# A fused layer's last down-projection as seven block products instead of eight, with its operands' sums made during the up-projections

## The chip, the core and the metric

The kernel runs on one core of a Trainium2 chip. Its engines run side by side: TensorE (PE, with PEld for its weight loads), VectorE (DVE), ScalarE (ACT), GpSimd (POOL) and SyncE (SP), which here issues every DMA between DRAM and the on-chip memory (SBUF). PE writes its results into PSUM banks of 128x512 fp32. The metric is the device time of one execution in microseconds (us), a median of several.

## The reference

One layer: a SwiGLU feed-forward block, two attentions with a merge, and a second SwiGLU block, for 1024 latent tokens of width 1024 (and 256 context tokens ahead of the second block). What the change touches is the second block, with 2816 inner columns:

```python
def _swiglu(h, w1, w3, w2):
    return (jax.nn.silu(h @ w1) * (h @ w3)) @ w2
...
x = _residual(x, _swiglu(_modnorm(x, g[4], m[6], m[7]), ffn2_w1[l], ffn2_w3[l], ffn2_w2[l]),
              g[5], m[8], HALF_STEP)
```

`_residual` normalises each token's row, multiplies by a gate row and adds `x`. All is fp32. To keep fp32's precision in PE's faster format (`fp32r`), each operand is split into a high part (an ACT cast) and the rest (a DVE subtraction), and each product is three matmuls: high by high, high by low, low by high (`mm3`, line 158).

## The kernel before

The **order** comes from a `Plan` (line 163): a list of main steps that hold the matmuls of a stage, and side steps that `spread` lays evenly behind a range of main steps. All engines take their instructions in the order in which this plan writes them. A `store` made in a main step is put on SP's queue two steps later (`waiting`, `flush`); a load goes on at once, and whatever stands in SP's queue is issued in order.

The **up-projections** of the second block (`up_units`, `Unit`, `plan_rest`) work on pairs of inner tiles of 128. For each pair there are two units, one for w1 and one for w3; 11 pairs make 22 units. Each unit multiplies a 2 x 2 block matrix of weights by one of tokens (h's halves) in seven products instead of eight, with sums of the weight blocks made by DVE (`sum`), splits of these by ACT and DVE, and results combined from PSUM banks by DVE. One product is one main step of 12 matmuls (4 inner steps of 3). The first 14 units are led: their products `first` and `second` are done earlier, and five products, p6, p5, p7, p3, p4, are left to them; the last 8 units have all seven. `plan_rest` thus has 14 x 5 + 8 x 7 = 126 main steps. The w1 unit's results go through a Silu on ACT (`emit1`), the w3 unit's are multiplied with them by DVE (`emit3`) and stored, by halves of 512 tokens, to the DRAM buffer `gd2` (one 128x1024 tile for each of the 22 inner tiles).

The **pools** concerned: `T2()` gives tiles of 128x512 from the pool `half`, which has 20; in the rows below they are named `t`. `xu` are tiles of the pool `units` (24), `xv` of the pool `wide` (16), `d` are DRAM buffers. The PSUM banks are `bs` (3), `bm` (3) and `bv` (2). A tile is given out again once its last reader is done, a DMA too.

The **down-projection** (`Down`, `groups`) works on groups of inner tiles, nine of two and one of four. For each tile it loads 512 KB of w2 and 512 KB of `gd2` and splits both. A main step `tile(t)` takes one token tile of 128 (8 of them) and both output halves `e`; for each it runs 3 matmuls per inner tile of the group into a bank:

```python
for x, f in enumerate(fs):
    mm3(pd, [y[:, c] for y in g[f]], self.w[f][e], x == 0, x == len(fs) - 1)
if fs[0] == 0:
    act.copy(ys[t][:, o], pd)
else:
    vec.tensor_tensor(ys[t][:, o], ys[t][:, o], pd, op=ALU.add)
```

So each of 10 groups ends with 16 evictions of 128x512: for the first group a copy by ACT, for the others an addition to `ys[t]` by DVE. Beside it run the steps of the last modulation column (`ada_steps((8,))`, 16 loads `in_wada` and 16 small matmuls), its gate rows (`last_gates`), and in the last group the residual of each token tile in two halves (`done2`: statistics, gate, the addition of `x2s`, the store of the output).

Of the kernel before, what the change touches and what calls it, by code (L numbers as in the profile page):

```python
# [43 lines left out]
def hybrid_block(ctx: ExitStack, tc: tile.TileContext, a: dict, out: bass.AP):  # L44
# [25 lines left out]
    def V(dt=F32):  # L70
        return U(dt, "v")
# [4 lines left out]
    def T2(dt=F32, n=512):  # L76
        return pools["t"].tile([P, n], dt, tag="t", name=nm("t"))
# [4 lines left out]
    def DR(shape):  # L82
        n = nm("d")
        return dp.tile(shape, F32, tag=n, name=n)
# [3 lines left out]
    def PB(tag):  # L88
        return ps.tile([P, 512], F32, tag=tag, name=nm("b" + tag), bufs=PBUFS[tag])
# [22 lines left out]
    class Engine:  # L112


        def __init__(self, e):
            self.e = e
# [93 lines left out]
    def load(src, n=1024, key="u"):  # L210
        r = U(key=key)[:, :n]
        ld(r, src)
        return r
# [133 lines left out]
    def gate_rows(col, key="u"):  # L347
        row = U(key=key)
        for h in range(2):
            pb = PB("s")  # L350
# [239 lines left out]
    def plan_rest(plan, units):  # L590

        for i, u in enumerate(units):
            o = len(plan.main)
            e = plan.step(*u.rest())
            at = lambda n: o + u.names.index(n)
            for n, f in (u.within() if i else []) + (units[i + 1].before() if i + 1 < len(units) else []):
                plan.spread([f], at(n), at(n) + 1)
            if i + 2 < len(units):
                plan.spread([lambda v=units[i + 2], x=x: v.load(x) for x in (2, 0, 1)], e - 3, e)
# [54 lines left out]
                plan.spread([f], at[t] + x, at[t] + x + 1)  # L654


    def up_units(h, w1, w3, gd):

        units = []

        def pair_(p):
            s = {}

            def emit1(i, ci, x, bank):
                s[i, ci] = T2() if bank else x
                act.activation(s[i, ci], x, AF.Silu)

            def emit3(i, ci, x, bank):
                y = s.pop((i, ci))
                vec.tensor_tensor(y, x, y, op=ALU.mult)  # L670
                store(gd[2 * p + i, :, ci * 512:(ci + 1) * 512], y)
# [1243 lines left out]
    def last_col():  # L1915
        cols["g8"] = gate_col(8, 5, 0, 0.5)

    def last_gates():
        cols["g8"] = gate_rows(cols["g8"], "v")
# [109 lines left out]
```

## Time and profile before

| | us |
|---|---|
| median of 3 runs | 2691.38 |
| lowest and highest run | 2686.49, 2692.72 |
| the profiled execution, span on the core | 2689.4 |
| rest of the second block's up-projections | about 2096 to 2439 |
| its down-projection, first to last matmul | 2438.94 to 2681.0 |

The page puts the profiled execution in 40 equal slices, each digit the busy share in tenths:

```profile
PE   7999999999999999999999999999999999999998
DVE  4777875586866676665457988885535777565876
PEclk9999999999999999999999999999999999999999
GB/s 289 153 170 136 149 107 118 145 168 108 159 116 97 224 209 155 154 268 216 232 295 258 258 99 75 75 17 198 71 110 184 137 130 114 71 94 195 118 94 125
```

A slice is 67 us; the second block's part discussed here is the last nine slices. PEclk is the clock that TensorE was granted, and GB/s what all DMA engines moved. In the groups of instructions that come later, a row gives line, engine, operation, output and inputs, shapes and count, then busy time and mean duration in ns, then the idle time of the engine just ahead of them with the engine that ended it. In a timeline a row starts with the start and the duration.

### The profile page before, as it was taken

What the parts mean: (1) busy time and instruction counts of PE and PEld (TensorE: products, weight loads), DVE (VectorE), ACT (ScalarE), POOL (GpSimd) and SP (SyncE); (2) the same over time, 40 slices, a digit from 0 to 9 for tenths busy, and PEclk for the clock granted to TensorE, in tenths of its full rate; (3) what the DMA queues carried; (4) which work ended last, traced back from release to release, by engine and by line L of the source; (5) the groups of instructions that cost most, each with busy time, mean ns of one, the idle gap of its engine ahead of it and who ended that gap; (6) DMA issues with size and microseconds to landing.
All of it is one profiled execution on the core that took longest, in us unless ns stands there. A gap on an engine that the chain in (4) does not pass through costs nothing.

```text
span 2689.4 us, 37823 instructions
## 1 busy us (share of the span) xinstructions
PE 2638.9 (98%) x13822; PEld 2259.5 (84%) x13822; DVE 1838.0 (68%) x3443; ACT 1136.2 (42%) x2168; POOL 230.8 (9%) x380
## 2 busy tenths in 40 slices
PE   7999999999999999999999999999999999999998
PEld 5888888888898788799888999997788888888887
DVE  4777875586866676665457988885535777565876
ACT  5522233522223753331447987773256322324111
POOL 0000000000000400000103532221020000000001
PEclk9999999999999999999999999999999999999999
DMA  7454433453432654476889942205235433225323
GB/s 289 153 170 136 149 107 118 145 168 108 159 116 97 224 209 155 154 268 216 232 295 258 258 99 75 75 17 198 71 110 184 137 130 114 71 94 195 118 94 125
DMA packets 186154, 409.69 MB, mean 152 GB/s; under 512 B 21680, under 2 KB 60784, under 8 KB 185968
## 3 DMA queue, kind: packets, MB, share of 16 engines
q1 hardware_dynamic: 185968, 407.27, 46.8%
q8 instruction: 109, 1.79, 0.3%
q14 instruction: 77, 0.63, 0.1%
HBM read 308.04 MB, written 99.16 MB: 151 GB/s over the span
## 4 chain that ended last, share of the span: by engine, by line
PE 52%; issue 33%; ACT 6%; DVE 6%; DMA 2%; POOL 1%; SPq 0%; DVEq 0%; POOLq 0%; ACTq 0%
PE bs L153 23%; PE bm L153 15%; PE bv L153 11%; PE bm L156 2%; ACT xu L1648 1%; DVE t L120 1%; DVE xu L1515 1%; DVE xu L120 1%; ACT xu L1549 1%; POOL st L120 1%; DVE xv L120 1%; ACT t L120 1%; ACT t L1674 1%; DVE t L1675 1%; ACT xu L120 1%
## 5 line engine op out<-in xcount | busy, mean ns | idle before, releaser
L153 PE MATMUL bm<-xu,xu 128*128 128x512 f32 (+2 forms) x2304 | 551.4, 388 | 1.4 <-DVE xu L120 1.1
L153 PEld LDWEIGHTS bm<-xu,xu 128*128 128x128 f32 x2304 | 426.0, 189 | 84.8 <-DVE xu L120 1.9
L153 PE MATMUL bs<-xu,xu 128*128 128x512 f32 (+1 forms) x1908 | 459.5, 386 | 0.6 <-DVE xu L120 0.4
L153 PEld LDWEIGHTS bs<-xu,xu 128*128 128x128 f32 x1908 | 354.6, 189 | 69.7 <-DVE xu L120 0.9
L153 PE MATMUL bs<-xv,xu 128*128 128x512 f32 (+1 forms) x1488 | 355.7, 389 | 4.7 <-DVE t L120 4.6
L153 PEld LDWEIGHTS bs<-xv,xu 128*128 128x128 f32 x1488 | 279.6, 189 | 62.2 <-issue 6.3
L153 PE MATMUL bv<-xv,xu 128*128 128x512 f32 x1276 | 318.5, 389 | 0.0
L120 ACT CAST xu<-t 128x512 fp32r<-128x512 f32 x248 | 150.8, 616 | 335.6 <-DVE t L120 332.9
L153 PEld LDWEIGHTS bv<-xv,xu 128*128 128x128 f32 x1276 | 239.6, 188 | 49.8
L120 DVE TENSOR_TENSOR xu<-t,xu 128x512 fp32r<-128x512 f32 x248 | 170.5, 689 | 136.3 <-ACT xu L120 136.3
L120 DVE TENSOR_TENSOR xu<-xv,xu 128x512 fp32r<-128x512 f32 (+2 forms) x244 | 182.8, 770 | 63.3 <-ACT xu L120 60.1
L120 POOL TENSOR_SCALAR st<-st 128x1 f32<-128x1 f32 x72 | 41.6, 577 | 2104.4 <-ACT t L120 2038.7
L153 PE MATMUL bs<-w,w 96*128 96x512 f32 (+3 forms) x832 | 206.1, 366 | 7.7 <-DVE st L1540 7.1
L120 DVE TENSOR_TENSOR xu<-xu,xu 128x512 fp32r<-128x512 f32 (+2 forms) x225 | 154.4, 692 | 76.8 <-ACT xu L120 74.7
L120 ACT CAST xu<-xv 128x512 fp32r<-128x512 f32 (+2 forms) x216 | 137.2, 694 | 125.4 <-DVE xv L120 108.6
L153 PE MATMUL bm<-t,xu 128*128 128x256 f32 (+1 forms) x1272 | 167.3, 289 | 0.6 <-ACT t L120 0.4
L153 PEld LDWEIGHTS bm<-t,xu 128*128 128x128 f32 x1272 | 162.3, 193 | 5.7 <-ACT t L120 0.8
L153 PE MATMUL bv<-xu,xu 128*128 128x512 f32 x596 | 160.4, 391 | 0.0
L153 PE MATMUL bv<-t,w 128*128 128x256 f32 x896 | 151.2, 288 | 5.0 <-ACT t L1674 1.7
L153 PEld LDWEIGHTS bv<-t,w 128*128 128x128 f32 x896 | 132.6, 189 | 20.6 <-DVE t L1675 5.0
L120 ACT CAST xu<-xu 128x512 fp32r<-128x512 f32 (+2 forms) x217 | 131.9, 621 | 29.2 <-DMA xu<-in_wc 18.1
L153 PEld LDWEIGHTS bs<-w,w 96*128 96x128 f32 (+1 forms) x832 | 123.2, 190 | 17.1 <-DVE st L1540 10.1
(187 smaller groups left out, 3674.8 us busy)
## 6 DMA issues: line engine op xcount, KB each, us to landing
d<-t SPq DMA_DIRECT2D x244, 256.0 KB, 2.4
xu<-in_f1w SPq DMA_DIRECT2D x64, 512.0 KB, 4.1
xv<-in_f1w SPq DMA_DIRECT2D x64, 512.0 KB, 3.7
xv<-d SPq DMA_DIRECT2D x62, 512.0 KB, 4.2
xu<-in_f2w SPq DMA_DIRECT2D x60, 512.0 KB, 3.9
t<-in_wada SPq DMA_DIRECT2D x112, 256.0 KB, 3.9
w<-d SPq DMA_DIRECT2D x112, 256.0 KB, 6.5
t<-d SPq DMA_DIRECT2D x76, 256.0 KB, 4.1
```

The source lines that it names most:

```text
L120: return lambda *x, **y: pin(f(*x, **y))
L153: return pin(nc.tensor.matmul(o, s, m, start=start, stop=stop, skip_group_check=open_group[0]))
L156: return pin(nc.tensor.transpose(o, x, i))
L1515: nc.vector.tensor_scalar(dst, src, 1.0, FMIN, op0=ALU.mult, op1=ALU.max, accum_out=m)
L1549: soft.append(lambda s=s: nc.scalar.activation(pr[s][:, :640], pr[s][:, :640], AF.Exp, bias=n_[:, s:s + 1], accum_out=l[:, s:s + 1]))
L1648: nc.scalar.activation(x, x, AF.Exp, bias=n_[:, s:s + 1], accum_out=l[:, i:i + 1])
L1674: nc.scalar.copy(t[0], pb)
L1675: nc.vector.tensor_tensor(t[1], pb, f32(t[0]), op=ALU.subtract)
```

## The change

The down-projection is written as the product of a 2 x 2 block matrix A (rows: token halves of 512; columns: even and odd inner tile of each pair) and a 2 x 2 block matrix W (rows: even and odd inner tile; columns: output halves of 512). It needs seven products of blocks: with s1 = a21 + a22, s2 = s1 - a11, s3 = a11 - a21, s4 = a12 - s2 and t1 = w12 - w11, t2 = w22 - t1, t3 = w22 - w12, t4 = w21 - t2, these are a11 w11, a12 w21, s2 t2, s1 t1, s4 w22, s3 t3 and a22 t4.

- `Quarters` holds the token blocks: where a w3 unit's result was stored to `gd2`, a11, a12 and a22 are now stored each to a buffer of its own, and a21 is kept. The four sums of a pair (one DVE operation and one store each) stand behind the steps p5, p7, p3, p4 of the next pair's w1 unit if that is led, else behind its second to fifth step. For the 7 led pairs a11 is loaded again (`back`) ahead of that. The last pair's sums stand in the down-projection's first steps.
- `WeightQuarters` loads for each pair the four blocks of w2 (256 KB each), makes t1 to t4 with four DVE subtractions and stores them: six side steps for each of 11 pairs, laid evenly over the 126 main steps but four.
- `Down7` has 77 steps (7 products by 11 inner steps), each with 4 token tiles of 3 matmuls, into four banks; operands are loaded six steps ahead (two pieces of 256 KB) and split three steps ahead. Products that are added to one another stay in their banks, so a bank is read after each product only: 28 evictions. The last 5 inner steps of the last product are done token tile by token tile (`tail`, 15 matmuls each), as before the last group.
- The modulation's steps, its gate rows and `done2` are placed anew; the gate rows use the banks `bv` instead of `bs`.

```diff
+    def plan_quarters(plan, quarters, p, o):
...
+        def run(x):
+            if not made:
+                made.extend(quarters.steps(p))
+            made[x]()
+        for x in range(4):
+            plan.spread([lambda x=x: run(x)], o + x + 1, o + x + 2)
...
+            if quarters:
+                if i % 2 and u.led:
+                    plan.spread([lambda p=i // 2: quarters.back(p)], o, o + 1)
+                elif i % 2 == 0 and i:
+                    plan_quarters(plan, quarters, i // 2 - 1, o)
...
+    class Quarters:
...
+        def take(self, p, i, ci, y):
+            n = "a" + "12"[ci] + "12"[i]
+            self.y[p][n] = y
+            if n != "a21":
+                store(self.d[n][p], y)
...
+        def back(self, p):
+            t = self.y[p]["a11"] = T2()
+            ld(t, self.d["a11"][p])
...
+            def s1():
+                y["s1"] = T2()
+                vec.tensor_tensor(y["s1"], y["a21"], y["a22"], op=ALU.add)
+                store(self.d["s1"][p], y["s1"])
+            def s3():
+                vec.tensor_tensor(y["a21"], y["a11"], y["a21"], op=ALU.subtract)
+                store(self.d["s3"][p], y["a21"])
+            def s2():
+                vec.tensor_tensor(y["a11"], y["s1"], y["a11"], op=ALU.subtract)
+                store(self.d["s2"][p], y["a11"])
+            def s4():
+                vec.tensor_tensor(y["a12"], y["a12"], y["a11"], op=ALU.subtract)
+                store(self.d["s4"][p], y["a12"])
+                self.y[p] = None
+            return [s1, s3, s2, s4]
...
+    class WeightQuarters:
...
+        def load(self, p):
+            for n in ("w11", "w12", "w22", "w21"):
+                t = self.r[p, n] = T2()
+                ld(t, self.src(n, p))
...
+        def sums(self, p):
+            w = {n: self.r.pop((p, n)) for n in ("w11", "w12", "w22", "w21")}
+            def one(n, x, y, out):
+                vec.tensor_tensor(w[out], w[x], w[y], op=ALU.subtract)
+                store(self.d[n][p], w[out])
+            return [lambda a=a: one(*a) for a in (("t1", "w12", "w11", "w11"), ("t3", "w22", "w12", "w12"),
+                                                  ("t2", "w22", "w11", "w22"), ("t4", "w21", "w22", "w21"))]
...
+                s += [lambda p=p: self.load(p), lambda: None] + [lambda x=x, run=run: run(x) for x in range(4)]
...
+    class Down7:
...
+        ORDER = (("a11", "w11"), ("a12", "w21"), ("s2", "t2"), ("s1", "t1"), ("s4", "w22"), ("s3", "t3"), ("a22", "t4"))
+        TAIL = 5
...
+        def load(self, i):
+            (a, w), k = self.ORDER[i // NP], i % NP
+            self.r[i] = T2(), T2()
+            ld(self.r[i][0], self.q.d[a][k])
+            ld(self.r[i][1], self.wq.src(w, k))
+        def split(self, i, x):
+            self.w.setdefault(i, []).append(split(self.r[i][x]))
+            if x:
+                self.r.pop(i)
...
+        def product(self, i, t):
+            open_group[0] = True
+            o, k = i // NP, i % NP
+            a, w = self.w[i]
+            mm3(self.banks[t], [x[:, t * P:(t + 1) * P] for x in a], w, k == 0 and o in (0, 2, 3), k == NP - 1)
...
+        def step(self, i):
+            o, k = i // NP, i % NP
+            if k == 0:
+                if o == 0:
+                    self.xb = self.banks = [PB(x) for x in "smsm"]
+                if o == 2:
+                    self.yb = self.banks = [PB(x) for x in "smvv"]
+                if o == 3:
+                    self.xb = self.banks = [PB(x) for x in "smsm"]
+                if o == 4:
+                    self.banks = self.xb
+                if o == 5:
+                    self.banks = self.yb
+            for t in range(4):
+                self.product(i, t)
+            self.w.pop(i)
+            if k == NP - 1:
+                for t in range(4):
+                    self.out(o, t)
+        def out(self, o, t):
+            b, lo, hi = self.banks[t], slice(0, 512), slice(512, 1024)
+            ys = self.ys
+            if o == 0:
+                ys[t + 4] = V()
+                act.copy(ys[t + 4][:, lo], b)
+            elif o == 1:
+                ys[t] = V()
+                act.copy(ys[t][:, lo], b)
+            elif o == 2:
+                vec.tensor_tensor(ys[t][:, hi], b, ys[t + 4][:, lo], op=ALU.add)
+            elif o == 3:
+                vec.tensor_tensor(ys[t + 4][:, hi], b, ys[t + 4][:, lo], op=ALU.add)
+            else:
+                y = (ys[t][:, hi], ys[t + 4][:, hi], ys[t + 4][:, lo])[o - 4]
+                vec.tensor_tensor(y, y, b, op=ALU.add)
+        def tail(self, t):
+            for i in range(self.n - self.TAIL, self.n):
+                self.product(i, t)
+            self.out(6, t)
+        def plan(self, plan, ahead=6, led=3):
+            o = len(plan.main)
+            plan.step(*[lambda i=i: self.step(i) for i in range(self.n - self.TAIL)])
+            e = len(plan.main)
+            plan.step(*[lambda t=t: self.tail(t) for t in range(4)])
+            for i in range(self.n):
+                at = o + i - led
+                if i >= self.n - self.TAIL:
+                    at = e - 2 * (self.n - i)
+                plan.spread([lambda i=i: self.load(i)], at - ahead + led, at - ahead + led + 1)
+                plan.spread([lambda i=i, x=x: self.split(i, x) for x in range(2)], at, at + 1)
...
+                if quarters:
+                    quarters.take(p, i, ci, y)
+                else:
+                    store(gd[2 * p + i, :, ci * 512:(ci + 1) * 512], y)
...
-    gd2 = DR([NF, P, NLAT])
-    units2 = up_units(h3, a["f2w1"], a["f2w3"], gd2)
+    quarters2, wq2 = Quarters(), WeightQuarters(a["f2w2"])
+    units2 = up_units(h3, a["f2w1"], a["f2w3"], None, quarters2)
...
-    plan_rest(plan, units2)
-    gs = groups((2,) * 9 + (4,))
+    rest2 = len(plan.main)
+    plan_rest(plan, units2, quarters2)
+    plan.spread(wq2.steps(), rest2, len(plan.main) - 4)
     ys2 = {}
-    downs2 = [Down(a["f2w2"], gd2, ys2, fs) for fs in gs]
-    o = len(plan.main)
-    plan.spread([lambda: downs2[0].loads(0, "u")], o - 9, o - 8)
-    plan.spread(downs2[0].steps(key="u"), o - 7, o)
+    down2 = Down7(quarters2, wq2, ys2, None)
+    o, tail = down2.plan(plan)
+    plan_quarters(plan, quarters2, NP - 1, o)
...
-    d2_at = len(plan.main)
-    for i, d in enumerate(downs2):
-        o = len(plan.main)
-        plan.step(*[lambda d=d, t=t: d.tile(t) for t in range(8)])
-        if i + 1 < len(downs2):
-            n = downs2[i + 1]
-            plan.spread([lambda n=n: n.loads(n.fs[0])], o - 1, o)
-            plan.spread(n.steps(), o + 1, o + 8)
-        else:
-            plan.spread([last_col], o - 3, o - 2)
-            plan.spread([last_gates], o - 1, o)
-            for t in range(8):
-                plan.spread([lambda t=t: done2(t, 0)], o + t, o + t + 1)
-                plan.spread([lambda t=t: done2(t, 1)], min(o + t + 1, o + 7), o + 8)
-    plan.spread(ada_steps((8,)), d2_at + 8, len(plan.main) - 20)
+    plan.spread(ada_steps((8,)), o + 1, o + 2 * NP - 3)
+    plan.spread([last_col], o + 2 * NP - 3, o + 2 * NP - 2)
+    plan.spread([last_gates], o + 2 * NP - 2, o + 2 * NP - 1)
+    for t in range(4):
+        plan.spread([lambda t=t, x=x: done2(t, x) for x in range(2)], o + 5 * NP + 2 * t, o + 5 * NP + 2 * t + 2)
+        plan.spread([lambda t=t: done2(t + 4, 0)], tail + t, tail + t + 1)
+        plan.spread([lambda t=t: done2(t + 4, 1)], min(tail + t + 1, tail + 3), tail + 4)
```

Three places show how instructions move. First DVE, in the rest of a led w1 unit, from a sum for p7's bank on. Names: `t` are half tiles, `bs` and `bv` banks, `xu` the split weights. Before:

```order
L120 TENSOR_TENSOR t_21539<-t_21539,bs_21505 128x512
L120 TENSOR_TENSOR t_21561<-xu_21502,t_21544 128x512
L120 TENSOR_TENSOR xu_21563<-t_21561,xu_21563 128x512
L120 TENSOR_TENSOR t_21518<-t_21518,bv_21526 128x512
L120 TENSOR_TENSOR xu_21582<-t_21544,xu_21582 128x512
L120 TENSOR_TENSOR t_21585<-xu_21502 128x512
L120 TENSOR_TENSOR t_21361<-t_21361,bs_21505 128x512
L120 TENSOR_TENSOR xu_21603<-t_21585,xu_21603 128x512
L120 TENSOR_TENSOR t_21621<-bs_21608,t_21462 128x512
```

After, at the same products of a led w1 unit one pair earlier:

```order
L120 TENSOR_TENSOR t_21361<-t_21361,bs_21327 128x512
L120 TENSOR_TENSOR t_21084<-t_21232,t_21084 128x512
L120 TENSOR_TENSOR t_21394<-xu_21322,t_21368 128x512
L120 TENSOR_TENSOR xu_21396<-t_21394,xu_21396 128x512
L120 TENSOR_TENSOR t_21340<-t_21340,bv_21348 128x512
L120 TENSOR_TENSOR t_21232<-t_21363,t_21232 128x512
L120 TENSOR_TENSOR xu_21416<-t_21368,xu_21416 128x512
L120 TENSOR_TENSOR t_21419<-xu_21322 128x512
L120 TENSOR_TENSOR t_21174<-t_21174,bs_21327 128x512
L120 TENSOR_TENSOR t_21127<-t_21127,t_21232 128x512
L120 TENSOR_TENSOR xu_21439<-t_21419,xu_21439 128x512
L120 TENSOR_TENSOR t_21370<-t_21372,t_21370 128x512
L120 TENSOR_TENSOR t_21459<-bs_21446,t_21280 128x512
```

Four rows are new. The three token sums s3, s2 and s4 (`t_21084`, `t_21232`, `t_21127`) stand between the products' bank reads (rows with `bs` or `bv`) and the splits (rows with `xu`) as listed; s1 is `t_21363`, four rows ahead of these. `t_21370<-t_21372,t_21370` is a weight difference.

Second PE, where the down-projection starts. Rows with x2 and x3 are as many matmuls of one form. Before, a bank gets two inner tiles (6 matmuls) and PE goes on to the other output half, with two token halves of a split weight:

```order
L153 MATMUL bm_23622<-xu_23496,xu_23539 128x512 x2
L153 MATMUL bm_23622<-xu_23496,xu_23540 128x512
L153 MATMUL bm_23622<-xu_23561,xu_23596 128x512 x2
L153 MATMUL bm_23622<-xu_23561,xu_23597 128x512
L153 MATMUL bv_23630<-xu_23519,xu_23539 128x512 x2
L153 MATMUL bv_23630<-xu_23519,xu_23540 128x512
L153 MATMUL bv_23630<-xu_23578,xu_23596 128x512 x2
L153 MATMUL bv_23630<-xu_23578,xu_23597 128x512
```

After, each inner step gives 3 matmuls to each of four banks, and comes back to the first:

```order
L153 MATMUL bs_23909<-xu_23853,xu_23850 128x512 x3
L153 MATMUL bm_23910<-xu_23853,xu_23850 128x512 x3
L153 MATMUL bs_23911<-xu_23853,xu_23850 128x512 x3
L153 MATMUL bm_23912<-xu_23853,xu_23850 128x512 x3
L153 MATMUL bs_23909<-xu_23877,xu_23874 128x512 x3
L153 MATMUL bm_23910<-xu_23877,xu_23874 128x512 x3
L153 MATMUL bs_23911<-xu_23877,xu_23874 128x512 x3
L153 MATMUL bm_23912<-xu_23877,xu_23874 128x512 x3
```

A bank that was closed after 6 matmuls now stays open for 11 or 22 inner steps. Over the whole program PE's rows go from 10885 to 10489, DVE's from 3114 to 3166, ACT's from 1902 to 1982 and SP's from 1207 to 1445.

Third SP's queue early in the down-projection, where `in_f2w` is w2, `d` a DRAM buffer (`d_19714` is `gd2`, `d_19715` holds a11) and `in_wada` the modulation's weights. Before:

```order
L132 DMA xv_23680<-d_19714 128x1024
L132 DMA xv_23781<-in_f2w 128x1024
L132 DMA xv_23783<-d_19714 128x1024
L132 DMA t_23803<-in_wada 128x512
L132 DMA xv_23843<-in_f2w 128x1024
L132 DMA xv_23845<-d_19714 128x1024
L132 DMA t_23847<-in_wada 128x512
L132 DMA t_23889<-in_wada 128x512
L132 DMA xv_23946<-in_f2w 128x1024
```

After:

```order
L132 DMA t_24091<-in_f2w 128x512
L132 DMA t_24095<-in_wada 128x512
L132 DMA d_19720<-t_23638 128x512
L132 DMA t_24116<-d_19715 128x512
L132 DMA t_24117<-in_f2w 128x512
L132 DMA t_24121<-in_wada 128x512
L132 DMA t_24124<-in_wada 128x512
L132 DMA t_24144<-d_19715 128x512
L132 DMA t_24145<-in_f2w 128x512
L132 DMA t_24149<-in_wada 128x512
```

Transfers of 128x1024 have become twice as many of 128x512, and the stores of the last sums stand among them.

More of the change, by code (lines that the diff above doesn't have):

```diff
@@ L588, in plan_leads, with plan_rest @@
         plan.step(*lead_main(units[:n]))
-    def plan_rest(plan, units):
+    def plan_quarters(plan, quarters, p, o):
+        made = []
+        def run(x):
[4 more added lines that the diff above has]
+            plan.spread([lambda x=x: run(x)], o + x + 1, o + x + 2)
+    def plan_rest(plan, units, quarters=None):
         for i, u in enumerate(units):
@@ L654, in plan_chains, with __init__, steps @@
                 plan.spread([f], at[t] + x, at[t] + x + 1)
-    def up_units(h, w1, w3, gd):
+    class Quarters:
+        def __init__(self):
+            self.d = {n: DR([NP, P, 512]) for n in ("a11", "a12", "a22", "s1", "s2", "s3", "s4")}
+            self.y = [{} for _ in range(NP)]
+        def take(self, p, i, ci, y):
[6 more added lines that the diff above has]
+            ld(t, self.d["a11"][p])
+        def steps(self, p):
+            y = self.y[p]
+            def s1():
[13 more added lines that the diff above has]
+            return [s1, s3, s2, s4]
@@ new lines, in hybrid_block, with __init__, src, steps @@
+    class WeightQuarters:
+        def __init__(self, w2):
+            self.w2 = w2
+            self.d = {n: DR([NP, P, 512]) for n in ("t1", "t2", "t3", "t4")}
+            self.r = {}
+        def src(self, n, p):
+            if n[0] == "t":
+                return self.d[n][p]
+            o = 512 * (int(n[2]) - 1)
+            return self.w2[2 * p + int(n[1]) - 1][:, o:o + 512]
+        def load(self, p):
[9 more added lines that the diff above has]
+                                                  ("t2", "w22", "w11", "w22"), ("t4", "w21", "w22", "w21"))]
+        def steps(self):
+            s = []
+            for p in range(NP):
+                made = []
+                def run(x, p=p, made=made):
+                    if not made:
+                        made.extend(self.sums(p))
+                    made[x]()
+                s += [lambda p=p: self.load(p), lambda: None] + [lambda x=x, run=run: run(x) for x in range(4)]
+            return s
@@ new lines, in hybrid_block, with __init__ @@
+    class Down7:
+        ORDER = (("a11", "w11"), ("a12", "w21"), ("s2", "t2"), ("s1", "t1"), ("s4", "w22"), ("s3", "t3"), ("a22", "t4"))
+        TAIL = 5
+        def __init__(self, q, wq, ys, done):
+            self.q, self.wq, self.ys, self.done = q, wq, ys, done
+            self.r, self.w = {}, {}
+            self.n = NP * len(self.ORDER)
+        def load(self, i):
[12 more added lines that the diff above has]
+            mm3(self.banks[t], [x[:, t * P:(t + 1) * P] for x in a], w, k == 0 and o in (0, 2, 3), k == NP - 1)
+            open_group[0] = False
+        def step(self, i):
[48 more added lines that the diff above has]
+                plan.spread([lambda i=i, x=x: self.split(i, x) for x in range(2)], at, at + 1)
+            return o, e
@@ L659, in up_units @@
+    def up_units(h, w1, w3, gd, quarters=None):
         units = []
```

7 lines of the change are left out of this document (3 added, 4 removed).

## The prediction

> **What bounds the kernel now.** First the page's top: the busy shares over the whole span.
>
> ```profile
> span 2689.4 us, 37823 instructions
> PE 2638.9 (98%) x13822; PEld 2259.5 (84%) x13822; DVE 1838.0 (68%) x3443; ACT 1136.2 (42%) x2168; POOL 230.8 (9%) x380
> ```
>
> The tensor engine (PE) is busy for 98%, but that is a mean over stages with different limits, so I read the windows of the stages that the change touches. The columns are: the window, its length, then busy time and count of PE, PEld, DVE, ACT and POOL, the granted clock, the DMA share, and GB/s.
>
> ```profile
> 2080.00:2160.00 80.00, 80.00 (x355) 66.26 (x354) 60.01 (x89) 27.57 (x45) 0.00 (x0) 1.00 0.43 142
> 2160.00:2220.00 60.00, 60.00 (x266) 49.73 (x265) 42.90 (x68) 17.34 (x31) 0.00 (x0) 1.00 0.35 114
> 2270.00:2420.00 150.00, 150.00 (x664) 124.24 (x663) 91.58 (x145) 45.04 (x80) 0.00 (x0) 1.00 0.25 83
> 2440.00:2495.00 55.00, 55.00 (x245) 45.54 (x244) 30.05 (x43) 25.43 (x40) 0.00 (x0) 1.00 0.59 206
> 2495.00:2600.00 105.00, 105.00 (x473) 87.25 (x472) 81.04 (x120) 21.45 (x30) 0.00 (x0) 1.00 0.34 111
> ```
>
> In the second FFN's up-projections (to about 2439 us) and its down-projection (after that) PE fills every window to the last digit at a granted clock of 1.00, while VectorE (DVE) has between 23% (81.04 of 105) and 45% (30.05 of 55) idle. The chain of waits says the same from the other side:
>
> ```profile
> 2436.22 2.72 PE bs L153 x12
> 2438.94 1.36 PE bm L153 x6
> 2440.30 1.36 PE bv L153 x6
> ...
> 2566.78 1.36 PE bm L153 x6
> ```
>
> It is nothing but matmuls, in pieces of 12 (one up-projection product) and, from 2438.94 us, of 6 (one output half of one token tile). The largest group of the down-projection's matmuls adds, in its last column, that they wait for nothing (0.0):
>
> ```profile
> L153 PE MATMUL bm<-xu,xu 128*128 128x512 f32 x380 | 95.8, 389 | 0.0
> ```
>
> Both give the price on which everything rests: 2.72/12 = 1.36/6 = **0.2267 us per matmul of 512 columns**, start to start. (The group's mean of one, 389 ns, is the duration of pipelined, overlapping matmuls, and is not used.) So this stage is bound by the number of matmuls, and every other engine counts only if it comes to be later than PE.
>
> **Term 1: the matmuls.** Before, each of 22 inner tiles is multiplied for 8 token tiles and 2 halves, each with 3 matmuls (the split product): 22 x 8 x 2 x 3 = 1056. After: 7 block products, each over 11 inner steps and 4 token tiles with 3 matmuls: 7 x 11 x 4 x 3 = 924. The form stays: 128x512 outputs, 128x128 stationary slices. That is 132 fewer, 132 x 0.2267 = **-29.9 us**. The small matmuls (16 for the last modulation column, 8 transposes) are in both.
>
> **Term 2: the sums beside the up-projections.** Added on DVE are 44 token sums and 44 weight differences of 128x512. Here is DVE before, in the part where the units are led (five products left per unit, 13.6 us):
>
> ```profile
> 2215.28 0.69 DVE L120 TENSOR_TENSOR xu<-t,xu 128x512 fp32r<-128x512 f32 x1 [0.77 <-ACT xu L120]
> 2215.94 0.69 DVE L120 TENSOR_TENSOR t<-t,bv 128x512 f32<-128x512 f32 x1
> 2217.84 0.69 DVE L120 TENSOR_TENSOR xu<-t,xu 128x512 fp32r<-128x512 f32 x1 [1.21 <-ACT xu L120]
> 2218.44 0.69 DVE L120 TENSOR_TENSOR t<-xu 128x512 f32<-128x512 f32 x1
> 2219.05 0.68 DVE L120 TENSOR_TENSOR t<-t,bs 128x512 f32<-128x512 f32 x1
> 2220.93 0.69 DVE L120 TENSOR_TENSOR xu<-t,xu 128x512 fp32r<-128x512 f32 x1 [1.21 <-ACT xu L120]
> 2221.54 0.68 DVE L120 TENSOR_TENSOR t<-bs,t 128x512 f32<-128x512 f32 x1
> 2222.14 0.68 DVE L120 TENSOR_TENSOR t<-xu,t 128x512 f32<-128x512 f32 x1
> 2222.74 0.68 DVE L120 TENSOR_TENSOR xu<-xu,xu 128x512 fp32r<-128x512 f32 x1
> 2224.10 0.69 DVE L120 TENSOR_TENSOR t<-bv,t 128x512 f32<-128x512 f32 x1 [0.67 <-PE bv L153]
> ```
>
> Operations that follow one another start 0.60 us apart, so 88 of them are 53 us of DVE. None of it reaches the end as long as DVE keeps up. Led part: 42.90 of 60 us is 71.5%; per pair of units (27.2 us) come 4 token sums and about 3.5 weight sums, 7.5 x 0.60 = 4.5 us or 17%: some **88%**. Unled part: 91.58 of 150 is 61%, with 38 us per pair 73%. The mean leaves room, so I go through the one tight place, a led w1 unit as its rows stand with the change. s1 and s3 stand ahead of a split's low part, where DVE waits 1.21 us for ACT anyway. s2 stands ahead of the read of p4's bank, which is not written again soon. s4 and, at worst, a weight difference stand ahead of the next unit's read of p6's bank. Such a read starts today as soon as PE is done (as the last row's does), so it comes 0.6 to 1.2 us late. p7 writes this bank again when p5 is through, 2.72 us after p6, and the read takes 0.69: 2.0 us are allowed. I cost the delay at 0; its cover is the 0.8 us that are left.
>
> **Term 3: splits and evictions in the down-projection.**
>
> ```profile
> L120 DVE TENSOR_TENSOR xv<-xv,bs 128x512 f32<-128x512 f32 x52 | 35.7, 687 | 21.4 <-PE bs L153 21.2
> L120 DVE TENSOR_TENSOR xu<-xv,xu 128x512 fp32r<-128x512 f32 x40 | 27.3, 686 | 10.3 <-ACT xu L120 10.3
> ...
> L120 DVE SCALAR_TENSOR_TENSOR t<-t,sc,t 128x512 f32<-128x512 f32 x14 | 10.5, 747 | 0.0
> ...
> L120 ACT CAST xu<-xv 128x512 fp32r<-128x512 f32 x40 | 23.7, 619 | 109.0 <-DVE xv L120 108.6
> L120 ACT COPY xv<-bs 128x512 f32<-128x512 f32 x8 | 4.6, 589 | 22.6 <-PE bs L156 18.6 <-PE bs L153 4.0
> ```
>
> Evictions fall from 160 to 28 (8 copies on ACT, 20 additions on DVE). Splits rise to 154 casts and 154 subtractions of 128x512, two per step. A step is 12 matmuls, 2.72 us; in it DVE has 2 x 0.60 = 1.2 us of splits and one piece of modulation work (0.75), together 1.95 of 2.72; ACT has 2 x 0.62 = 1.24 us of casts. They stand three steps (8.2 us) ahead of their use. Where four banks are evicted and written again at once, a copy of 0.59 or addition of 0.69 us meets banks that PE writes 4 x 0.68 = 2.72 us per round: 2.0 us remain. Cost 0.
>
> **Term 4: DMA.** Before there were 44 loads of 512 KB and 44 stores of 256 KB (34.6 MB). After, all in pieces of 256 KB: 77 token stores, 7 reloads, 44 weight loads, 44 weight stores, 154 operand loads, 326 in all (85.5 MB). All go through SP's one queue.
>
> ```profile
> xu<-in_f2w SPq DMA_DIRECT2D x43, 512.0 KB, 3.7
> d<-t SPq DMA_DIRECT2D x38, 256.0 KB, 2.0
> t<-d SPq DMA_DIRECT2D x14, 256.0 KB, 3.3
> ```
>
> These are the up-projections' rows (count, size, median us from issue to landing). One of the down-projection's first 56 us and two of its densest windows:
>
> ```profile
> t<-in_wada SPq DMA_DIRECT2D x11, 256.0 KB, 5.0
> ...
> 2442.00:2447.00 5.00, 5.00 (x24) 4.14 (x23) 0.69 (x1) 2.57 (x5) 0.00 (x0) 1.00 0.92 320
> 2447.00:2452.00 5.00, 5.00 (x24) 4.14 (x23) 1.27 (x2) 3.71 (x6) 0.00 (x0) 1.00 1.03 415
> ```
>
> In the rest of the up-projections 128 pieces are added, 33.6 MB in 126 products (343 us), 98 GB/s on top of the 83 to 142 of the windows: at most 240, against 320 and 415 in the last two rows here. The down-projection is denser at first: in 19 steps (51.7 us) 38 operand loads, 16 modulation loads and about 8 stores of 0.262 MB, 16.2 MB, or **313 GB/s**. Those two rows lie at and above it. Loads are issued six steps (16.3 us) ahead and landed in 3.3 to 5.0 us, so I take 0; the upper end is in rival C. The Trainium skill, "Perfetto Trace Analysis", section "DMA Optimizations", speaks against the change here: larger transfers use the engines better, and rows shrink from 4 KB to 2 KB. Rows of 2 KB (the t<-d line) landed in 3.3 us here against 3.7 us for the 512 KB pieces, so half the bytes took nearly as long and the trace agrees in direction; with the loads 16.3 us ahead the sum is the same by rule and row, and only the time of rival C hangs on it.
>
> **Term 5: the end.** The last matmul hands over to a chain that stays as it is:
>
> ```profile
> 2681.08 0.69 DVE L120 TENSOR_TENSOR xv<-xv,bs 128x512 f32<-128x512 f32 x1 [1.82 <-PE bs L153]
> 2681.69 1.28 DVE L120 SCALAR_TENSOR_TENSOR xv<-xv,st,xv 128x1024 f32<-128x1024 f32 x1
> 2681.87 1.06 ACT L120 ACTIVATE t<-xv 128x1024 bf16<-128x1024 f32 x1 [4.29 <-DVE xv L120]
> ...
> 2682.88 1.22 DVE L120 TENSOR_TENSOR xv<-xv,xv 128x1024 f32<-128x1024 f32 x1
> ...
> 2684.82 1.41 DVE L120 SCALAR_TENSOR_TENSOR xv<-xv,st,xv 128x512 f32<-128x512 f32 x2 [0.72 <-POOL st L120]
> ```
>
> From 2681.08 to the span's end at 2689.4 are 8.3 us. The last tiles now come 15 matmuls (3.40 us) apart instead of 24 (5.44). DVE has 0.61 + 1.28 + 1.22 = 3.1 us per tile in these rows, still less. A delay of one operation is possible: 0 to 1.3 us, taken as 0.5, nearer to the row in which DVE is on time.
>
> **The sum.** On the profiled execution's span: 2689.4 - 29.9 + 0.5 = 2660.0. The runs' median, 2691.4, stands 2.0 above that span: 2691.4 - 29.9 + 0.5 = **2662.0 us**, 1.1% less. By the Trainium skill, "TensorE: Matmul & The Clock Gate", section "Wait — 56ns, not 53.3ns?", 512 columns take 512/2.4 + 2.5 = 215.8 ns back to back, and the gain would be 28.5 us (2663.4); the chain's row says 226.7, and the row decides.
>
> **The rivals.**
> - **B, DVE falls behind in the led part.** At 88% the wait for ACT (1.21 us in the rows above) or for a store before a half tile is overwritten (2.0 us landing) may no longer fit. A late bank read then holds PE by up to one landing per pair: 7 led pairs x 2.0 = 14 us. For it: the 0.8 us of margin; against it: 12% idle, and the w3 unit between has no token sums, so lags don't add up. 2662 to 2677.
> - **C, the queue is late at the start of the down-projection.** If 16.2 MB flow no faster than the 206 GB/s that stage had as a mean, they take 78.6 us instead of 51.7, +27 us; with the 320 GB/s row 50.6 us, nothing. So 2662 to 2689. Against it: 206 was what was asked, not a limit, and the loads may run ahead.
> - **D, no gain.** PE is not what sets the end, or the time comes back wholly: 2686 to 2697. The windows at 55.00 of 55 and 105.00 of 105 speak against it.
> - **E, slower.** The 20 half tiles run out. About 11 live there before; now a11, s1, a12, a21, a22 and four weight pieces of a pair are added, which makes 20. If a weight load for the next unit must wait in SP's queue for a tile held by a pair's sums, everything behind it waits too, the unit's own weights among it. It turns slower than before once that wait exceeds 29.9/11 = 2.72 us per pair; at one load under pressure (5.0 us) per pair it is 55 us, +25: about 2716. Against it: the stores free the tiles 2.0 us after a sum, and their next use in program order lies at least four products (10.9 us) behind.
>
> **Chances.** Forecast (2656 to 2668, with the ±3 us by which runs of before differ): 63%. B: 17%. C: 8%. D: 4%. E: 5%. More gain than the matmuls: 3%. The range 2656 to 2676 holds A, most of B and half of C, near 82%. Some 0.2% (5.4 us) is what a measurement of this kernel can tell from no change; faster by more than that has A, B, nearly all of C and the last case, 91%; the same 4%; slower 5%.
>
> **What would show it.** Step 1: 924 matmuls of 128x512 after the last up-projection, pieces of 12 at 2.72 us in the chain, about 210 us from its first to its last. Step 2: PE without waits in the up-projections, DVE near 88% and 73%; otherwise a "PE waits for DVE" row at a w1 unit. Step 3: no PE idle "<-DVE xu" in the down-projection. Step 4: 300 GB/s and more in its first 52 us, and no "<-DMA" behind the casts that reaches PE. Step 5: 8.3 to 9.6 us from the last addition to the end. The forecast is wrong if PE waits more than some 6 us in the stage, wherever it does.

## The result, and the profile after

| | before | after | with both cuts (below) |
|---|---|---|---|
| median of the runs, us | 2692.05 (4 runs) | 2674.65 (4 runs: 2671.72 to 2677.34) | 2664.07 (4 runs) |
| ratio to before | | 0.9939 (0.9925 to 0.9953) | 0.9897 (0.9882 to 0.9912) |
| span of the profiled execution | 2689.4 | 2672.9 | 2660.1 |
| from the last transposition ahead of the second block to the last addition | 629.01 | 612.34 | 599.99 |

The last column stands against its own runs of before (median 2691.36). The last row is the yardstick of this text. The kernels here have the same program up to the second block, and yet their profiled executions reach its start up to 4.8 us apart (2049.18 to 2053.95 in all traces but that with 19 half tiles); this stretch leaves that out. Four kernels without the stall have it at 599.98 to 600.01. It goes from the start of the row "PE L156 MATMUL bs<-ident,xv ... x4" (2052.07 us before, 2052.33 after) to the last row of DVE that reads a bank (2681.08 and 2664.67).

The whole kernel takes 0.6% less, and the interval is clear of 1. The change saved 16.7 us in this stretch, where the matmuls alone were worth 29.9. The view of what PE waited for, from 2040 us on, names the rest (releaser, us in total, times, longest). Before, it had no row in that window; after:

```profile
PE bs L153 <- DVE xv L120: 8.5, 1, 8.5
PE bs L153 <- DVE xu L120: 1.3, 1, 1.3
PE bs L153 <- DVE t L120: 0.4, 1, 0.4
```

Windows put them in their places (columns as in the prediction):

```profile
2160.00:2220.00 60.00, 60.00 (x266) 49.69 (x265) 52.14 (x85) 17.39 (x30) 0.00 (x0) 1.00 0.68 232
...
2270.00:2420.00 150.00, 149.62 (x660) 123.33 (x658) 113.25 (x182) 44.33 (x79) 0.00 (x0) 1.00 0.51 175
...
2440.00:2495.00 55.00, 55.00 (x252) 45.85 (x251) 39.75 (x68) 25.45 (x44) 0.00 (x0) 1.00 0.97 351
...
2600.00:2640.00 40.00, 30.21 (x124) 24.20 (x123) 26.70 (x39) 17.02 (x28) 1.70 (x3) 0.87 0.81 280
```

The up-projections are as full as before but for 0.4 us, and so are the first 160 us of the down-projection, at 351 GB/s in its first 55 us. Nearly everything is lost between 2600 and 2640 us: PE is busy for 30.2 of 40. Finer windows show two losses, the wait and what follows it:

```profile
2620.00:2625.00 5.00, 3.95 (x18) 2.94 (x16) 1.93 (x4) 1.86 (x3) 0.00 (x0) 1.00 1.00 349
2625.00:2630.00 5.00, 0.00 (x0) 0.00 (x0) 3.18 (x5) 1.82 (x3) 0.00 (x0) 0.64 0.35 132
2630.00:2635.00 5.00, 2.54 (x6) 2.09 (x7) 5.00 (x9) 1.85 (x3) 0.00 (x0) 0.50 0.97 294
2635.00:2640.00 5.00, 5.00 (x20) 3.98 (x20) 5.00 (x9) 4.29 (x7) 0.00 (x0) 0.84 1.05 395
```

After the wait the granted clock is 0.50, and 12 matmuls take 4.78 us (2632.46 to 2637.24) instead of 2.72. So 8.5 + 1.3 + 2.1 = 11.9 us are accounted for.

Where the waits come from is told by the timeline of all engines there (start, duration, engine, operation; in brackets the idle time ahead and what ended it):

```profile
2606.40 1.28 DVE L120 SCALAR_TENSOR_TENSOR xv<-xv,st,xv 128x1024 f32<-128x1024 f32 x1 [3.74 <-DMA xv<-d]
...
2607.03 1.22 ACT L120 CAST xu<-t 128x512 fp32r<-128x512 f32 x2 [2.75 <-DMA t<-d]
...
2607.72 0.34 SPq L132 DMA_DIRECT2D out_x<-xv  x1
2608.15 2.21 SPq L132 DMA_DIRECT2D t<-d  x4
...
2610.41 0.42 SPq L132 DMA_DIRECT2D xv<-d  x1
```

The next round, from the window behind it:

```profile
2615.90 1.28 DVE L120 SCALAR_TENSOR_TENSOR xv<-xv,st,xv 128x1024 f32<-128x1024 f32 x1 [4.67 <-DMA xv<-d]
2616.51 1.22 ACT L120 CAST xu<-t 128x512 fp32r<-128x512 f32 x2 [1.43 <-DMA t<-d]
...
2617.21 0.34 SPq L132 DMA_DIRECT2D out_x<-xv  x1
2617.64 2.18 SPq L132 DMA_DIRECT2D t<-d  x4
```

This is a round of `done2` for token tiles 0 to 3, which the change set two main steps (5.44 us) apart amid the last products. SP issues in order. The store `out_x` waits for DVE's last addition (the row "xv<-xv,st,xv"); that waits for the residual load `xv<-d`; and that load stands in SP's queue behind four operand loads (2.2 us) and the store of the round before. So 2607.72 to 2617.21 is 9.5 us: 2.7 until the residual load is issued, 5.5 until DVE starts on it, 1.3 for DVE. The stores came at 2599.15, 2607.72, 2617.21 and 2628.13 us. The operand loads behind each store come late too, and ACT's casts wait for them ("<-DMA t<-d").

What held PE itself is DVE, which stood still for the residual loads. The rows that end in the long wait:

```profile
2621.07 0.84 PE L153 MATMUL bs<-xu,xu 128*128 128x512 f32 x3
...
2626.82 1.28 DVE L120 SCALAR_TENSOR_TENSOR xv<-xv,st,xv 128x1024 f32<-128x1024 f32 x1 [4.90 <-DMA xv<-d]
...
2628.02 3.69 DVE L120 TENSOR_TENSOR xu<-t,xu 128x512 fp32r<-128x512 f32 x6
...
2631.64 0.68 DVE L120 TENSOR_TENSOR xv<-xv,bs 128x512 f32<-128x512 f32 x1
...
2632.46 1.62 PE L153 MATMUL bs<-xu,xu 128*128 128x512 f32 x3 [8.51 <-DVE xv L120]
```

The matmuls at 2621.07 are product 6's last on the bank `bs`, and product 7 goes on in the same banks, so PE may write there only when DVE has read them. That read (2631.64) stands in DVE's order behind the fourth tile's residual, which waited 4.90 us for its load, and behind six splits. It comes 10.6 us after those matmuls began; in the kernel with both edits (below) it comes 0.9 us after (2619.04 to 2619.92). The 1.3 us wait is of the same kind: PE wants a split (2617.10 us) that DVE makes only behind the third tile's residual (2615.90 us).

Before, the same rounds stood in the last group, with no operand load behind them any more; the residual load went out right behind the store, and the rounds were 5.4 us apart:

```profile
2650.36 0.34 SPq L132 DMA_DIRECT2D out_x<-xv  x1
2650.78 0.38 SPq L132 DMA_DIRECT2D xv<-d  x1
2655.80 0.34 SPq L132 DMA_DIRECT2D out_x<-xv  x1
```

The end is as forecast: the last rows of DVE, 3.40 us apart, and 8.2 us to the span's end at 2672.9.

```profile
2661.27 0.69 DVE L120 TENSOR_TENSOR xv<-xv,bv 128x512 f32<-128x512 f32 x1 [0.38 <-PE bv L153]
...
2664.67 0.69 DVE L120 TENSOR_TENSOR xv<-xv,bv 128x512 f32<-128x512 f32 x1 [0.38 <-PE bv L153]
```

### The profile page after: what moved, and what is told of

It reads as the page before. It is cut to its first block, busy times and chain, and to the rows that moved or that the text cites. A ratio compares the mean times of both kernels' runs of the same rounds, so it can differ in the third digit from the quotient of the medians.

```text
span 2672.9 us, 38325 instructions
## 1 busy us (share of the span) xinstructions
PE 2612.1 (98%) x13690; PEld 2235.5 (84%) x13690; DVE 1847.6 (69%) x3495; ACT 1173.5 (44%) x2248; POOL 229.5 (9%) x380
## 5 line engine op out<-in xcount | busy, mean ns | idle before, releaser
L153 PE MATMUL bm<-xu,xu 128*128 128x512 f32 (+1 forms) x2271 | 553.9, 388 | 1.4 <-DVE xu L120 1.1
L153 PEld LDWEIGHTS bm<-xu,xu 128*128 128x128 f32 x2271 | 420.2, 189 | 84.2 <-DVE xu L120 1.9
L153 PE MATMUL bs<-xu,xu 128*128 128x512 f32 (+1 forms) x1875 | 462.5, 386 | 10.6 <-DVE xv L120 8.5
L120 ACT CAST xu<-t 128x512 fp32r<-128x512 f32 x402 | 239.5, 618 | 407.4 <-DVE t L120 333.7
L153 PEld LDWEIGHTS bs<-xu,xu 128*128 128x128 f32 x1875 | 348.3, 189 | 79.1 <-issue 8.9
L120 DVE TENSOR_TENSOR xu<-t,xu 128x512 fp32r<-128x512 f32 x402 | 265.8, 686 | 142.8 <-ACT xu L120 142.8
L120 DVE TENSOR_TENSOR xu<-xv,xu 128x512 fp32r<-128x512 f32 (+2 forms) x184 | 131.3, 738 | 48.2 <-ACT xu L120 45.0
L120 DVE TENSOR_TENSOR t<-t,t 128x512 f32<-128x512 f32 (+2 forms) x222 | 142.3, 643 | 25.8 <-ACT t L120 23.0
L153 PE MATMUL bv<-xu,xu 128*128 128x512 f32 x530 | 144.2, 393 | 0.0
```

What stands on the lines that cost most here:

```text
L120: return lambda *x, **y: pin(f(*x, **y))
L153: return pin(nc.tensor.matmul(o, s, m, start=start, stop=stop, skip_group_check=open_group[0]))
```

## The experiments

The theory (L, the loop through SP's queue) was set against a full DMA system (Q: share 0.81 in those 40 us), and against a DVE with too much to do there (V). The first four runs share a chip and its runs of before; the first two cut the loop, each at another link. The first three were executed four times, each of the others once.

**The residual load earlier**, in front of the loop:

```diff
+    def load_xr(t):
+        cols["xr", t] = V()
+        ld(cols["xr", t], x2s[t * P:(t + 1) * P, :])
     for t in range(4):
+        plan.spread([lambda t=t: load_xr(t)], o + 5 * NP + 2 * t - 6, o + 5 * NP + 2 * t - 5)
```

> Only the four loads of the residual rows (x2s) of token tiles 0 to 3 move: they are issued 6 main steps ahead of their use instead of one. Theory L (a loop through SP's queue): in the changed kernel each store of an output tile stands in SP's queue ahead of later operand loads and waits for DVE's last addition, which waits for the residual load (5.5 us), which was issued behind the store before; one round takes 8.6 to 10.9 us where the plan has 5.44, four rounds use up the six steps that the loads are ahead, and PE waits 1.3 + 8.5 us and then runs 12 matmuls 2.1 us slower. With the load early the loop is cut: no PE wait over 0.5 us after 2440 us, span 2672.9 - 11.9 = 2661.0 (2660 to 2662). Rival Q (the DMA engines are full there, share 0.81): same bytes in the same time, so waits stay, 2671 to 2674. Rival V (DVE has too much work there, 4.9 of 5.44 us per tile): waits shrink to about a half, 2666 to 2670.

Measured: ratio 0.9895 (0.9880 to 0.9910), span 2662.2, stretch 600.01 us. No wait of PE is left but the 0.4 us of the up-projections, and 55 us that had the stall are full:

```profile
2595.00:2650.00 55.00, 55.00 (x244) 45.53 (x244) 40.79 (x57) 25.84 (x45) 11.42 (x9) 1.00 0.54 192
```

The span is 1.2 above the expectation because this execution began the second block 1.6 us later than that of the changed kernel.

**The output store later:**

```diff
-                store(out[t * P:(t + 1) * P, o:o + n], z[:, o:o + n], 0)
+                store(out[t * P:(t + 1) * P, o:o + n], z[:, o:o + n], 0 if t >= 4 else 3)
```

> Only the four stores of the output of token tiles 0 to 3 move: they enter SP's queue three main steps later. Theory L: the loop is cut at its other link, since operand loads no longer stand behind a store that waits for DVE; no PE wait over 0.5 us after 2440 us, span 2661.0 (2660 to 2663; DVE may still wait for a residual load, but nothing behind it is late). Rival Q: same bytes, 2671 to 2674. Rival V: DVE has the same work at the same steps, 2668 to 2674.

Measured: ratio 0.9896 (0.9880 to 0.9913), span 2661.5, stretch 599.99 us. Either cut alone brings back the whole 12.3 us, with the same bytes (against Q) and the same work on DVE (against V). It also settles a rival that was not named, a residual load that is issued too late whatever the queue does: here it is still issued one step ahead, and DVE has no wait for it left between 2590 and 2640 us.

**Both edits together:**

> Residual loads of tiles 0 to 3 six steps earlier and their output stores three steps later, together. Theory L: one cut is enough, so no more than either alone: span 2661.0 (2660 to 2662), about 0.989 of the kernel before. Rival Q: 2671 to 2674. Rival V: 2666 to 2670.

Measured: ratio 0.9897 (0.9882 to 0.9912), span 2660.1, stretch 599.99: nothing more, as L has it. With either cut, or with both, the kernel is faster than before and than the changed one.

**Rounds further apart**, `o + 5 * NP + 3 * t` in place of `2 * t`:

> The residual steps of token tiles 0 to 3 stand 3 main steps apart (8.16 us) instead of 2 (5.44); loads and stores keep their places relative to them. Theory L: a round of 8.6 to 9.5 us is then late by 0.4 to 1.3 us each instead of 3.2 to 5.5; four rounds stay within the cover, PE waits under 1 us, span 2661 to 2662.5, while DVE still waits 4 to 5 us for each residual load. Rival Q: fewer bytes per time, 2664 to 2670. Rival V: DVE has 3.9 of 5.44 us, no waits, about 2661, and DVE no longer waits for the residual loads for long.

Measured: span 2663.2, stretch 605.33, one wait of PE of 3.4 us, again for DVE's read of product 6's banks (and a clock of 0.80 in the 5 us behind it). Under 1 us was expected: that took the round as given. SP's rows show that it grows with the spacing, since six operand loads instead of four now stand between a store and the next residual load:

```profile
2605.90 0.34 SPq L132 DMA_DIRECT2D out_x<-xv  x1
...
2609.94 0.42 SPq L132 DMA_DIRECT2D xv<-d  x1
...
2617.68 0.34 SPq L132 DMA_DIRECT2D out_x<-xv  x1
```

That is 4.0 us to the load and 11.8 us for the round, against a plan of 8.16. More room for the loop loosens it but doesn't break it.

**Less cover**, on the changed kernel: `plan(self, plan, ahead=4, led=3)`.

> The changed kernel itself, with the down-projection's operands loaded 4 main steps ahead instead of 6 (split still 3 ahead). Theory L: the four late rounds through SP's queue (8.6 to 10.9 us for 5.44) use up the cover that the loads have; two steps less are 5.4 us less cover, so PE waits there 9.8 + 5.4 = 15.2 us (14 to 17) instead of 9.8, beginning a round earlier, and the span is 2677 to 2681. Elsewhere in the down-projection nothing waits, since a load lands after 5.2 us and its product is 10.9 us away. If the cover in steps does not matter (SP far ahead anyway), the waits stay 9.8 and the span 2673.

Measured: span 2673.7, stretch 616.32, which is 4.0 us more than the changed kernel; PE waits 13.0 us there.

```profile
PE bs L153 <- ACT xu L120: 12.5, 3, 10.3
PE bs L153 <- DVE xu L120: 0.5, 2, 0.2
PE bs L153 <- DVE t L120: 0.4, 1, 0.4
```

The direction is that of L, and the stall begins earlier and in three pieces; 3.2 us more wait for two steps less is under the 5.4 expected. The stores came in rounds of 9.4, 8.9 and 10.3 us here and of 8.6, 9.5 and 10.9 there, so part of the size lies in how long each round takes; the rest I have not traced.

**Another issuer for the stores.** The Trainium skill, "Perfetto Trace Analysis", section "DMA Optimizations", says that it may make sense to give loads to one issuing engine and stores to another. Two runs of the changed kernel do so for the four stores:

```diff
-                store(out[t * P:(t + 1) * P, o:o + n], z[:, o:o + n], 0)
+                if t < 4:
+                    pin(nc.gpsimd.dma_start(out[t * P:(t + 1) * P, o:o + n], z[:, o:o + n]))
+                else:
+                    store(out[t * P:(t + 1) * P, o:o + n], z[:, o:o + n], 0)
```

> The changed kernel with one edit: the output stores of token tiles 0 to 3 are issued by GpSimd at their old places instead of by SP; all loads stay on SP in their order. Theory L: SP no longer stands still behind DVE's last addition, the loop is cut as with the later stores, PE waits under 0.5 us in the down-projection, which takes 212 us from its first to its last matmul instead of 224.3; span 2660 to 2663. Rival Q (the DMA engines are full): the same bytes at the same time, 224 us stay.

> The same, with these four stores issued by ACT. Theory L: SP is free and loads come on time, so DVE does not wait for a residual load for more than 1 us; ACT stands at each store until DVE's addition is done, 1 to 3 us, and its casts have 8.2 us of cover: 212 us from the first to the last matmul, span 2660 to 2663. Rival A (a queue that waits for DVE hurts wherever it stands, since ACT's casts feed PE as SP's loads do): the casts come late in place of the loads, 216 to 224 us.

Measured: by GpSimd span 2661.2 and stretch 599.98, the loop is gone. By ACT (`nc.scalar`) span 2666.5 and stretch 605.54: PE waits 3.6 us, and the view of ACT's waits from 2585 us on shows its casts behind the stores:

```profile
ACT xu L120 <- DVE xv L120: 11.8, 3, 6.2
ACT xu L120 <- DMA t<-d: 5.0, 1, 5.0
```

So the advice helped in full with GpSimd, behind whose stores nothing stands that PE needs; on ACT, whose casts feed PE, a part of the wait only changed its seat. DVE's splits wait there for the late casts, and PE for the bank read behind these splits (rival A: 217.5 us from the first to the last matmul, at the low end of its range).

Three runs look at the terms that the prediction had set at nothing, all on top of both cuts.

**Weight differences beside the last 8 units only** (`rest2 + 5 * LEAD2` in place of `rest2`):

> On top of both cuts: all weight differences are made beside the last 8 units (56 products), none beside the 14 led ones. If the 0.9 us lost in the up-projections come from a weight difference behind s4 in a led w1 unit, the stretch of 387.6 us becomes 386.8 to 387.2, DVE falls from 87% to about 79% in the led part and rises from 76% to about 85% in the unled part. If the token sums alone make it late, 387.6 stays.

Measured: stretch 600.15; to the down-projection's first matmul it is 387.8 us, so the 386.8 to 387.2 expected were missed. In the windows DVE is at 81% in the led part (48.59 of 60) and 84% in the unled (125.58 of 150). The 0.4 us wait is gone from the view of PE's waits, so it did need the weight differences; but in the unled part matmuls now start late at seven places between 2310 and 2426 us, by 0.07 to 0.3 us each, too little for a row. Nothing is gained.

**Four more DVE operations per pair** beside s2 and s4:

```diff
                 vec.tensor_tensor(y["a11"], y["s1"], y["a11"], op=ALU.subtract)
+                vec.tensor_tensor(y["a11"], y["s1"], y["a11"], op=ALU.subtract)
+                vec.tensor_tensor(y["a11"], y["s1"], y["a11"], op=ALU.subtract)
```

> On top of both cuts: four more DVE subtractions for each pair (s2 undone and made again, twice), beside the second sum s2 and the fourth, s4, in the w1 unit; the values stay. From the last transposition ahead of the second block to the first matmul of its down-projection the kernel before takes 386.7 us and the one with both cuts 387.6. Theory M (the read of p6's bank behind s4 has under 1 us of cover): 4 x 0.60 = 2.4 us more ahead of that read make it late in most of the 7 led pairs, PE waits 0.4 to 1.6 us in each, and the stretch becomes 390 to 399 us. Theory N (only DVE's mean load counts, 88% and 9% more are 97%): no more than 388.1.

Measured: stretch 616.88, 16.9 us more than without (404.5 us to the down-projection's first matmul). From 2040 us on PE waits:

```profile
PE bs L153 <- DVE t L120: 6.2, 6, 1.8
PE bm L153 <- ACT t L120: 4.1, 4, 1.2
PE bm L153 <- ACT xu L120: 1.8, 4, 0.8
```

Six led pairs wait for DVE at p6's bank, 1.0 us each on the average: the place and size of theory M, and not N. What I had not expected is that the four unled pairs wait too, and for ACT, whose Silu and casts come late behind DVE; the sum is beyond the 3 to 11 us expected. The three rows add up to 12.1 of the 16.9 us, and the rest has no row.

**One half tile less** (`TBUFS = 19`):

> On top of both cuts: 19 half tiles in the pool instead of 20. By the reckoning of the prediction (a half tile is given out again four products, 10.9 us, behind its last use, and a store lands in 2.2 us) one tile less changes nothing in the stretch of 387.6 us (within 0.5). By rival E (the pool is at its edge and SP stands still for a tile) it costs a landing of 2 to 5 us per pair, 410 us and more; the first block, which uses the same pool, may change too and is read apart.

Measured: stretch 599.97 and 387.6, unchanged, so the pool isn't at its edge in the second block. The span is 2674.3 all the same: the last transposition ahead of the second block starts 14.1 us later than in the run with both edits and 20 tiles, well over the 4.8 us by which the others differ.

```profile
2065.95 0.60 PE L156 MATMUL bs<-ident,xv 128*128 128x128 f32 x4
```

So the same pool seems to be at its edge earlier in the program, in parts that the change doesn't touch; where is not known.

## Why the prediction was right, and where it was not

The forecast of a gain held, and the time (2674.65) lies in the range (2656 to 2676), near its upper end. But that is luck. It lies outside the likeliest case's own range (2656 to 2668), in the part that was kept for rivals B and C, and the loss that brought it there is neither of them; it happens to be as large as theirs might have been. By the prediction's own sign, a wait of PE of more than some 6 us, its path was wrong: PE waits 9.8 us.

- **Term 1, the matmuls: right.** The page counts 132 fewer (13822 before, 13690 after). With the loop cut the stretch is 629.01 - 29.92 + 0.90 = 599.99 us, to the hundredth what the trace has; 0.90 is term 2.
- **Term 2, the sums at no cost: nearly right, with one delay mis-sized.** DVE came to 87% (52.14 of 60) and 75.5% (113.25 of 150), where 88% and 73% were forecast. (The 73% took 7.5 sums for an unled pair as for a led one; the differences are laid evenly over time, so 38 us hold five of them, and nine sums of 0.60 us give 75%.) The place was right too. In the last led pair s4 and the read of p6's bank came so late that p7 waited:

```profile
2277.68 0.69 DVE L120 TENSOR_TENSOR t<-t,t 128x512 f32<-128x512 f32 x1
...
2278.28 0.68 DVE L120 TENSOR_TENSOR t<-bs,t 128x512 f32<-128x512 f32 x1
...
2279.11 3.00 PE L153 MATMUL bs<-xv,xu 128*128 128x512 f32 x12 [0.39 <-DVE t L120]
```

  The read came 2.3 us after p6 was through (2276.0 us), where the prediction had 0.6 to 1.2 us and a limit of 2.0. From the last transposition to the down-projection's first matmul it is 387.61 us (2052.33 to 2439.94) for 386.71 before (2052.07 to 2438.78): 0.90 us. Rival B had this place, at 14 us; the doubled sums show that it decides as soon as DVE has 2.4 us more per pair.
- **Term 3, splits and evictions: right only as long as DVE is on time.** Outside the stalled 40 us nothing in the down-projection waits for one. Inside, both waits of PE ended with one: a split (1.3 us) and the bank read ahead of product 7 (8.5 us), for which the term had "2.0 us remain". The work on DVE was not the cause, as it is the same in the runs without the wait; the term left out that DVE can stand still for a load.
- **Term 4, the DMAs: the bytes were right, the order was not looked at.** 351 GB/s in the first 55 us (313 forecast) with loads landing after 5.2 us delayed nothing, so rival C, a full queue, fell, and so did E with 19 half tiles.

```profile
t<-d SPq DMA_DIRECT2D x38, 256.0 KB, 5.2
t<-in_wada SPq DMA_DIRECT2D x16, 256.0 KB, 5.2
```

  What failed is the step "Loads are issued six steps (16.3 us) ahead and landed in 3.3 to 5.0 us, so I take 0". Six steps is their place in the program; in SP's queue four stores stood ahead of them that wait for DVE. Nor are all loads six steps ahead: the residual loads of tiles 0 to 3 are one step ahead, stand in the same queue, and are the ones that DVE, and PE behind it, stood for. The prediction followed `done2` only into the tail, for tiles 4 to 7, and gave the four rounds of tiles 0 to 3 amid the products no line: the store, what it waits for, and what is queued behind it. That is 12.3 us, 11.9 of them seen as waits and the slow clock.
- **Term 5, the end: right**, with the allowance of 0.5 not needed (8.2 us for 8.3).
- **The clock was left out.** A wait of 8.5 us cost 2.1 us more afterwards. The Trainium skill, "TensorE: Matmul & The Clock Gate", section "What's actually happening", states that an idle window of about 3.4 us throttles the array to half; the granted 0.50 agrees, and so does the 1.3 us wait at 2617 us, behind which the clock stayed at 1.00.

With the cut made, the ratio of 0.9897 is 27.7 us of 2691.4 (its interval 23.7 to 31.8), and the forecast of 29.4 lies in it.

## What to carry to other kernels

When a step is moved to a place amid other work, write down for each DMA that it issues what the DMA waits for and which loads stand behind it on its queue: one store that waits for an engine holds up every load behind it, however many steps ahead the program puts them. If the waiting engine itself waits for a load on the same queue, that is a loop, and here its round (8.6 to 10.9 us), not the engines' busy shares nor the bandwidth, set the pace. Whatever the waiting engine does next is late as well, here a bank read that PE needed. Cutting one link (the load earlier, the store later, or a queue behind which nothing needed stands) was enough; spreading the rounds from 5.44 to 8.16 us was not.

## What was not expected of the hardware

The clock fell after waits of PE of 3.4 us (granted 0.80 in the 5 us behind it, with the rounds further apart) and of 8.5 us (0.50), but not after 1.3 us, nor after 1.8 us (the longest wait with the four more operations, where the windows of that stage show 1.00). So here a stall past some point between 1.8 and 3.4 us cost about 2 us more than its own length: 605.33 - 599.99 = 5.3 us in all for the wait of 3.4, and 605.54 - 599.99 = 5.6 us for the 3.6 us with the stores on ACT.
